# Hybrid decoder, attention stage: two value sums of a head in one PSUM bank, evacuated together

## The chip, the cores and the metric

One core of one Trainium2 chip runs the whole program. The metric is the device time of one execution in microseconds (us). PE is TensorE, DVE is VectorE, ACT is ScalarE, POOL is GpSimd, SP is SyncE, which here issues nearly all transfers.

## What is computed

Two decoder layers on 1024 tokens of width 1024. In each layer one input projection feeds four token mixers of 256 columns; their outputs `y` go through one output projection and a layer norm, then a SwiGLU and a second layer norm. Two of the mixers, a dilated sliding-window attention (c) and a latent attention (b), are computed as masked softmax attention, four heads each:

```
y_a = _gmlp_mixer(z_a, ...)
y_b = _mla_mixer(z_b, positions, ...)
y_c = _dilated_mixer(z_c, positions)
y_d = _mlstm_mixer(z_d, ...)
y = jnp.concatenate([y_a, y_b, y_c, y_d], axis=-1) @ w_out[l]
x = _layer_norm(DEEPNORM_ALPHA * x + y, ln1_g[l], ln1_b[l])
...
s = jnp.where(key_pos[None, :] <= q_pos[:, None], s, -jnp.inf)
p = jax.nn.softmax(s, axis=-1).astype(v.dtype)
return jnp.einsum('bhqk,bkhd->bqhd', p, v)
```

## The kernel before

Float32 products are made from two parts, a rounded high part and the remainder (`PH` and `PL`, `wh` and `wl`): ACT casts the high part, DVE or POOL subtracts it.

`attn` treats four head pairs in turn: `G[0]`, `G[1]` are the heads of mixer c, `G[2]`, `G[3]` those of mixer b. For each head (`hh`) and each block of 128 queries (`i`), `scores` makes score tiles `sc` on PE; DVE adds the mask while it reduces (L824, `P` and `mn`); ACT takes the exponential (L828); POOL scales by the reciprocal of the sum (L831). `turn` transposes `P` on PE (`pt`) and splits it (ACT `PH`, DVE `PL`). `values` makes the value sum `pv` of a block of 256 queries (`jp`, 0 to 3) on PE. The blocks come in the order jp 0, 3, then 1, 2, with jp 0 or 1 first and its partner soon after. The rows 0 to 63 of `pv` come from the high part of V, the rows 64 to 127 from the remainder.

What becomes of `pv` differs by pair:

- `G[0]` to `G[2]`: ACT copies it to `tmp` (L886, 128x256) and SP sends its two halves to `yp` in HBM (L889, 64 KB each).
- `G[3]`: ACT copies the upper half (L883, 64x256) and DVE adds the lower half from PSUM into `Yb` (L884, 64x256).

PSUM has 8 banks of 512 columns: 3 carry the tag `mm`, 2 `s` (scores), 3 `t` (transposes). Tiles of a tag take its banks in turn. Under `mm` stand `pv`, the projections `pkb` and `pqb` that make keys and queries of the next pairs (`kst`, `q`) within the attention, and `po` of the output projection. A tile can be written only when all readers of the bank's last tile are done.

`out_proj` follows. `ysplit` brings the mixers' outputs back: for g = 0 and 3 it loads `yr` from `ys` (L1192), for g = 1 and 2 it loads both parts from `yp` (L1199), and DVE adds them (L1202, `yr<-yr`). ACT and POOL or DVE split each into `yT` (L146, L149). The `yr` tiles, and the raw tiles of `wO` ahead of them, share two buffers (pool `r`), so a load waits until the tile two before it has been split. `proj` then makes `po` in eight tiles of 128 tokens for each half of the columns.

The order on PE within the attention is as the code is written; the order on DVE, ACT, POOL and SP, and everything in `out_proj`, is set by the framework's scheduler from what each step costs and what it hands on, and so can move when an instruction is merged.

Of the kernel before, what the change touches and what calls it, by code (L numbers as in the profile page):

```python
# [11 lines left out]
ALU = mybir.AluOpType  # L12
# [46 lines left out]
class Net:  # L59
# [740 lines left out]
    def attn(self, groups):  # L800

        nc = self.nc

        rows = [(G, jp, hh, 2 * jp + e) for G in groups for two in ((0, 3), (1, 2)) for hh in range(2) for e in range(2) for jp in two]
        P_, PHL, norms = {}, {}, []

        def scores(n):
            G, jp, hh, i = rows[n]
            kst, q1, q2 = G["qk"]
            mask, scale, R, QR, pp = G["mask"], G["scale"], G.get("R"), G.get("QR"), G["pp"]  # L810
            nk = (i + 1) * 128
            qs = slice(i * 128, (i + 1) * 128)
            P = P_[n] = self.u("P", F32, pp[n % len(pp)])
            mn = self.sm("mn", 4)
            nch = (nk + 511) // 512
            for ch in range(nch):
                k0, k1 = ch * 512, min(nk, ch * 512 + 512)
                sp = self.psum("sc", "s")
                pairs = [(q1[hh][:, qs], kst[hh][:, k0:k1]), (q2[hh][:, qs], kst[hh][:, k0:k1])]
                if R is not None:  # L820
                    pairs.append((QR[i // 4][:, hh, (i % 4) * 128:(i % 4) * 128 + 128], R[:, k0:k1]))
                self.mms(sp[:, 0:k1 - k0], pairs)
                m0 = (7 - i) * 128 + k0
                nc.vector.tensor_tensor_reduce(out=P[:, k0:k1], in0=sp[:, 0:k1 - k0], in1=mask[:, m0:m0 + k1 - k0], scale=-scale,  # L824
                                               scalar=mn[:, ch - 1:ch] if ch else 3.0e38, op0=ALU.add, op1=ALU.min, accum_out=mn[:, ch:ch + 1])
            m = mn[:, nch - 1:nch]
            rs = self.sm("rs", 2)
            nc.scalar.activation(P[:, 0:nk], P[:, 0:nk], AF.Exp, scale=-1.0, bias=m, accum_out=rs[:, 0:1])  # L828
            def norm():
                nc.vector.reciprocal(rs[:, 1:2], rs[:, 0:1])  # L830
                nc.gpsimd.tensor_scalar(out=P[:, 0:nk], in0=P[:, 0:nk], scalar1=rs[:, 1:2], scalar2=1.0, op0=ALU.mult, op1=ALU.mult)  # L831
            norms.append(norm)
            while len(norms) > NLAG:
                norms.pop(0)()

        def turn(n):
            G, jp, hh, i = rows[n]
            key = (id(G), jp, hh)
            full = G["full"][jp]
            if i % 2 == 0:  # L840
                ng = (2 * jp + 5) // 4
                PHL[key] = [[self.u(s, F32 if full else F32R, "w").rearrange("p (b n) -> p b n", b=4) for _ in range(ng)] for s in (("PT",) if full else ("PH", "PL"))]
            P = P_.pop(n)
            for b0 in range(0, i + 1, 4):
                k = min(4, i + 1 - b0)
                pt = self.psum("pt", "t")
                for b in range(k):
                    nc.tensor.transpose(pt[:, b * 128:(b + 1) * 128], P[:, (b0 + b) * 128:(b0 + b + 1) * 128], self.ident)  # L848
                c0 = (i % 2) * 128
                src = pt[:, 0:k * 128].rearrange("p (b n) -> p b n", b=k)  # L850
                dst = [Pt[b0 // 4][:, 0:k, c0:c0 + 128] for Pt in PHL[key]]
                if full:
                    G["turns"] = G.get("turns", 0) + 1
                    (nc.scalar.copy if full[G["turns"] % len(full)] == "A" else nc.vector.tensor_copy)(dst[0], src)
                else:
                    self.split(*dst, src)

        def values(n):
            G, jp, hh, i = rows[n]
            V = G["V"]  # L860
            full = G["full"][jp]
            nb = 2 * jp + 2
            pv = self.psum("pv", "mm")
            pairs = PHL.pop((id(G), jp, hh))
            if "heads" in G:
                v = lambda b: V[b // 2][:, b % 2, G["heads"] + hh, :]
            elif full:
                v = lambda b: V[2][:, b, hh * 64:(hh + 1) * 64]
            else:
                v = lambda b: V[hh][:, b, :]  # L870
            m = 64 if full else 128
            for b in range(nb):
                c0 = 128 if b == nb - 1 else 0
                for x, Pt in enumerate(pairs):
                    nc.tensor.matmul(pv[0:m, c0:256], lhsT=v(b), rhs=Pt[b // 4][:, b % 4, c0:256],  # L875
                                     start=b == 0 and x == 0, stop=b == nb - 1 and x == len(pairs) - 1)
            tmp = self.t2("tmp", 256)
            if "Y" in G:
                y = G["Y"][64 * hh:64 * hh + 64, jp * 256:(jp + 1) * 256]
                if full:  # L880
                    nc.scalar.copy(y, pv[0:64, 0:256])
                else:
                    nc.scalar.copy(tmp[0:64, :], pv[0:64, 0:256])  # L883
                    nc.vector.tensor_tensor(out=y, in0=tmp[0:64, :], in1=pv[64:128, 0:256], op=ALU.add)  # L884
                return
            nc.scalar.copy(tmp[0:m, :], pv[0:m, 0:256])  # L886
            for part in range(2):
                dst = G["spill"][part][64 * hh:64 * hh + 64, jp * 256:(jp + 1) * 256]
                nc.sync.dma_start(dst, self.io["c_zero"][:, 0:256] if full and part else tmp[64 * part:64 * part + 64, :])  # L889

        NG = 16
        with self.tc.manual_schedule(engines=MAN):
            s = 0

            def ahead(n):
                nonlocal s
                while s < len(rows) and s <= n + rows[s][0]["ahead"]:
                    if s % NG == 0:
                        self.fill(999)
                        rows[s][0]["start"]()  # L900
                    scores(s)
                    left = sum(r[3] + 1 for r in rows[s:s - s % NG + NG])
                    self.fill(-(-len(self.jobs) * (rows[s][3] + 1) // left))
                    s += 1

            ahead(-1)
            for n in range(len(rows) + VLAG):
                m = n - VLAG
                for x in SEQ:
                    if x == "s":  # L910
                        ahead(n)
                        if s == len(rows):
                            while norms:
                                norms.pop(0)()
                    elif x == "t" and n < len(rows):
                        turn(n)
                    elif x == "v" and m >= 0 and rows[m][3] % 2 == 1:
                        values(m)
# [863 lines left out]
```

## Time and profile before

| what | value |
|---|---|
| time before, median of 3 runs (lowest to highest) | 2399.78 us (2398.84 to 2403.02) |
| the profiled execution, its own time | 2400.5 us |
| its span, mean granted clock of TensorE | 2398.8 us, 0.996 |
| PE busy | 2346.0 us (98%) |
| DVE, POOL, ACT busy | 1612.9 (67%), 1176.9 (49%), 1004.8 (42%) us |
| attention, first layer | 279 to 437 us of the span |
| attention, second layer | 1475 to 1633 us |

The span is the stretch from the first to the last instruction. The shares are means over stages: PE is near its end of what it can do over the whole, but not in the two attention stretches. [...]

### The profile page before, as it was taken

The numbers are of one execution on the slowest core, as the hardware profiler recorded it, in microseconds if no ns is written. First come the engines' busy times: TensorE is split into PE (matmuls) and PEld (weight loads), VectorE is DVE, ScalarE is ACT, GpSimd is POOL, SyncE is SP. The second block draws the span as 40 slices with busy tenths as digits, with TensorE's granted clock in tenths as the row PEclk, the third lists the DMA queues.
The fourth block names the chain that finished last, engine by engine and source line by source line (L and its number), as shares of the span: only waits on it lengthen the run. The fifth ranks groups of instructions, "written<-read, shape, count | busy, mean of one in ns | idle before, by whom it ended". The sixth has DMA issues, their size and how long they took to land.

```text
span 2398.8 us, 33440 instructions
## 1 busy us (share of the span) xinstructions
PE 2346.0 (98%) x11804; PEld 1971.7 (82%) x11804; DVE 1612.9 (67%) x2925; ACT 1004.8 (42%) x2004; POOL 1176.9 (49%) x1097
## 2 busy tenths in 40 slices
PE   9999999999999999999999999999999999999998
PEld 9789878777888888888897898788778888888886
DVE  7743588478765566767957435784787665667689
ACT  6323578334332323544343225783343323235442
POOL 2223525373545455767622244253735455547676
PEclk9999999999999999999999999999999999999999
DMA  4201112522332324653222110135213333345521
GB/s 169 65 29 43 31 37 83 186 110 70 115 114 87 113 99 170 216 189 101 93 66 64 36 37 31 38 87 188 110 62 114 116 102 107 108 164 208 189 97 70
DMA packets 91446, 246.81 MB, mean 103 GB/s; under 512 B 12096, under 2 KB 18560, under 8 KB 91280
## 3 DMA queue, kind: packets, MB, share of 16 engines
q1 hardware_dynamic: 91280, 244.68, 30.1%
q8 instruction: 94, 1.54, 0.3%
q14 instruction: 72, 0.59, 0.1%
HBM read 180.64 MB, written 64.52 MB: 102 GB/s over the span
## 4 chain that ended last, share of the span: by engine, by line
PE 82%; DVE 9%; issue 3%; ACT 3%; POOL 2%; DMA 1%; SPq 0%; POOLq 0%; ACTq 0%; DVEq 0%
PE gu L124 34%; PE dn L124 14%; PE zc L124 6%; PE po L124 5%; PE zvo L572 4%; PE zdq L524 3%; PE za L124 3%; PE zb L124 3%; PE pv L875 2%; PE sc L124 2%; PE dl L124 2%; DVE P L824 1%; PE pt L848 1%; DVE x L1136 1%; DVE PL L149 1%
## 5 line engine op out<-in xcount | busy, mean ns | idle before, releaser
L124 PE MATMUL gu<-T,fc 128*128 128x512 f32 x2640 | 625.9, 395 | 5.1 <-DVE T L1374 5.1
L124 PEld LDWEIGHTS gu<-T,fc 128*128 128x128 f32 x2640 | 496.7, 188 | 123.3 <-DVE T L1374 6.6
L1279 POOL TENSOR_TENSOR fc<-fw,fc 128x512 fp32r<-128x512 f32 x232 | 325.5, 1406 | 348.8 <-ACT fc L1278 341.9
L124 PE MATMUL dn<-dc,dc 128*128 128x512 f32 x1512 | 352.2, 395 | 0.0
L124 PEld LDWEIGHTS dn<-dc,dc 128*128 128x128 f32 x1512 | 283.7, 188 | 68.3 <-DVE dc L1279 1.0
L1278 ACT CAST fc<-fw 128x512 fp32r<-128x512 f32 x232 | 142.8, 620 | 349.5 <-PE gu L124 218.5
L124 PE MATMUL gu<-B,fc 128*128 128x512 f32 x1056 | 260.0, 396 | 0.0
L124 PEld LDWEIGHTS gu<-B,fc 128*128 128x128 f32 x1056 | 197.6, 188 | 46.6
L149 POOL TENSOR_TENSOR dc<-hr,dc 128x512 fp32r<-128x512 f32 x126 | 190.1, 1520 | 79.4 <-ACT dc L146 69.9
L1437 DVE TENSOR_TENSOR Ra<-Ra,gu 128x512 f32<-128x512 f32 x172 | 117.6, 684 | 118.6 <-PE gu L124 101.8
L831 POOL TENSOR_SCALAR P<-P,rs 128x256 f32<-128x256 f32 (+7 forms) x128 | 95.8, 752 | 152.4 <-DVE rs L830 94.9
L124 PE MATMUL po<-wh,yT 128*128 128x512 f32 x512 | 163.2, 397 | 0.6 <-DVE x L1218 0.6
L124 PE MATMUL zc<-wh,xT 128*128 128x384 f32 x512 | 134.1, 339 | 0.0
L1278 ACT CAST dc<-dr 128x512 fp32r<-128x512 f32 x108 | 67.0, 622 | 129.9 <-PE dn L124 75.1
L124 PEld LDWEIGHTS po<-wh,yT 128*128 128x128 f32 x512 | 95.8, 188 | 23.4 <-DVE x L1218 1.5
L124 PE MATMUL sc<-kst,q 128*128 128x512 f32 (+3 forms) x384 | 107.7, 375 | 6.7 <-DVE mn L824 6.6
L828 ACT ACTIVATE P<-P,mn 128x256 f32<-128x256 f32 (+7 forms) x128 | 99.9, 782 | 21.4 <-DVE mn L824 19.8
L1279 DVE TENSOR_TENSOR dc<-dr,dc 128x512 fp32r<-128x512 f32 x72 | 81.1, 1136 | 35.4 <-ACT dc L1278 35.4
L149 DVE TENSOR_TENSOR PL<-pt,PH 128x512 fp32r<-128x512 f32 (+3 forms) x176 | 95.6, 557 | 12.3 <-ACT PH L146 11.8
L140 POOL TENSOR_TENSOR wl<-raw,wh 128x768 fp32r<-128x768 f32 (+2 forms) x32 | 62.6, 1962 | 79.6 <-ACT wh L132 79.1
L124 PE MATMUL po<-wl,yT 128*128 128x512 f32 x256 | 100.7, 395 | 0.0
L848 PE MATMUL pt<-ident,P 128*128 128x128 f32 x576 | 89.2, 281 | 11.4 <-DVE PL L149 5.7
(393 smaller groups left out, 4896.3 us busy)
## 6 DMA issues: line engine op xcount, KB each, us to landing
fw<-in_wGU SPq DMA_DIRECT2D x88, 512.0 KB, 4.6
hr<-hs SPq DMA_DIRECT2D x142, 256.0 KB, 2.8
dr<-in_wD SPq DMA_DIRECT2D x44, 512.0 KB, 5.2
hs<-Ra SPq DMA_DIRECT2D x40, 512.0 KB, 2.9
hs<-Rb SPq DMA_DIRECT2D x22, 512.0 KB, 5.5
raw<-in_wO SPq DMA_DIRECT2D x16, 512.0 KB, 3.6
x<-x SPq DMA_DIRECT2D x16, 512.0 KB, 2.6
raw<-in_wC SPq DMA_DIRECT2D x16, 384.0 KB, 3.0
```

Source lines behind the costliest of these rows:

```text
L124: self.nc.tensor.matmul(out, lhsT=a, rhs=b, start=first and j == 0, stop=last and j == n - 1)
L140: (eng or nc.gpsimd).tensor_sub(lo[:, :n], raw[:, :n], f32(hi[:, :n]))
L149: (lo_eng or nc.vector).tensor_sub(lo, src, f32(hi))
L524: step(lambda: nc.tensor.matmul(pz, lhsT=a, rhs=b_, start=n == 0, stop=n == 23))
L572: nc.tensor.matmul(box["p"], lhsT=a, rhs=b_, start=j == 0, stop=j == 23)
L828: nc.scalar.activation(P[:, 0:nk], P[:, 0:nk], AF.Exp, scale=-1.0, bias=m, accum_out=rs[:, 0:1])
L831: nc.gpsimd.tensor_scalar(out=P[:, 0:nk], in0=P[:, 0:nk], scalar1=rs[:, 1:2], scalar2=1.0, op0=ALU.mult, op1=ALU.mult)
L848: nc.tensor.transpose(pt[:, b * 128:(b + 1) * 128], P[:, (b0 + b) * 128:(b0 + b + 1) * 128], self.ident)
L875: nc.tensor.matmul(pv[0:m, c0:256], lhsT=v(b), rhs=Pt[b // 4][:, b % 4, c0:256], start=b == 0 and x == 0, stop=b == nb - 1 and x == len(pa ...
L1278: nc.scalar.copy(dst[:, 0:512], src)
L1279: lo_eng.tensor_sub(dst[:, 512:1024], src, f32(dst[:, 0:512]))
L1437: tt = lambda o, a, b, op: v.tensor_tensor(out=o, in0=a, in1=b, op=op)
```

## The change

For `G[1]`, `G[2]` and `G[3]` the first block of a head (jp 0 or 1) writes the columns 0 to 255 of a new `pv` tile and returns; its partner (jp 3 or 2) writes the columns 256 to 511 of the same tile and evacuates both: one ACT copy of 512 columns, then two transfers of 64x2x256 (`G[1]`, `G[2]`) or one DVE add of 64x512 (`G[3]`). For one layer these are 12 tiles in place of 24, 12 ACT copies in place of 24, 16 transfers of 128 KB in place of 32 of 64 KB, and 4 DVE adds in place of 8. `G[0]` stays as it is.

```
-            pv = self.psum("pv", "mm")
+
+            both = not any(G["full"])
+            if both:
+                second = jp >= 2
+                if not second:
+                    open_pv[0] = self.psum("pv", "mm")
+                pv = open_pv[0][:, 256 * second:256 * second + 256]
+            else:
+                pv = self.psum("pv", "mm")
...
+            if both:
+                if not second:
+                    return
+                pv, tmp = open_pv[0], self.t2("tmp")
+                blocks = lambda x: x.rearrange("p (j n) -> p j n", n=256)
+                if jp == 3:
+                    at = lambda x: blocks(x)[:, 0:4:3, :]
+                else:
+                    at = lambda x: blocks(x)[:, 1:3, :]
+                if "Y" in G:
+                    nc.scalar.copy(tmp[0:64, :], pv[0:64, :])
+                    nc.vector.tensor_tensor(out=at(G["Y"][64 * hh:64 * hh + 64, :]), in0=blocks(tmp[0:64, :]), in1=blocks(pv[64:128, :]), op=ALU.add)
+                    return
+                nc.scalar.copy(tmp, pv)
+                for part in range(2):
+                    nc.sync.dma_start(at(G["spill"][part][64 * hh:64 * hh + 64, :]), blocks(tmp[64 * part:64 * part + 64, :]))
+                return
             tmp = self.t2("tmp", 256)
-            if "Y" in G:
-                y = G["Y"][64 * hh:64 * hh + 64, jp * 256:(jp + 1) * 256]
-                if full:
-                    nc.scalar.copy(y, pv[0:64, 0:256])
-                else:
-                    nc.scalar.copy(tmp[0:64, :], pv[0:64, 0:256])
-                    nc.vector.tensor_tensor(out=y, in0=tmp[0:64, :], in1=pv[64:128, 0:256], op=ALU.add)
-                return
```

Three places show how it moves instructions. The first is DVE near the end of the first layer's attention, where the first `yr<-yr` add stands (`P`, `mn`: the score reductions; the line L1202 of before is L1219 of after). Of before:

```order
L884 TENSOR_TENSOR Yb_4021<-tmp_4806,pv_4801 64x256
L149 TENSOR_TENSOR PL_4810<-pt_4811,PH_4809 128x128
L824 ISA P_4815,mn_4816<-sc_4817,maskB_4019 128x384
L824 ISA mn_4816 128x1
L1202 TENSOR_TENSOR yr_5203<-yr_5203 128x512
L830 RECIPROCAL rs_4797<-rs_4797 128x1
L830 RECIPROCAL rs_4822<-rs_4822 128x1
L884 TENSOR_TENSOR Yb_4021<-tmp_4843,pv_4826 64x256
L824 ISA P_4863,mn_4864<-sc_4865,maskB_4019 128x512
L824 ISA mn_4864 128x1
```

and of the changed kernel at the same place:

```order
L149 TENSOR_TENSOR PL_4767<-pt_4768,PH_4766 128x128
L1219 TENSOR_TENSOR yr_5147<-yr_5147 128x512
L824 ISA P_4772,mn_4773<-sc_4774,maskB_4005 128x384
L824 ISA mn_4773 128x1
L830 RECIPROCAL rs_4757<-rs_4757 128x1
L896 TENSOR_TENSOR Yb_4007<-tmp_4799,pv_4761 64x2x256
L830 RECIPROCAL rs_4779<-rs_4779 128x1
L824 ISA P_4819,mn_4820<-sc_4821,maskB_4005 128x512
L824 ISA mn_4820 128x1
```

The add of `yr` now stands ahead of the reduction of 384 columns (`P_4815` of before, `P_4772` of after). The second is POOL at the same time, where the scalings of `P` and the remainders of the first two `yT` stand. Of before:

```order
L831 TENSOR_SCALAR P_4760<-P_4760,rs_4767 128x256
L149 TENSOR_TENSOR yT_5197<-yr_5195,yT_5197 128x512
L149 TENSOR_TENSOR yT_5200<-yr_5195,yT_5200 128x512
L831 TENSOR_SCALAR P_4785<-P_4785,rs_4797 128x1024
L831 TENSOR_SCALAR P_4815<-P_4815,rs_4822 128x384
```

and now:

```order
L831 TENSOR_SCALAR P_4720<-P_4720,rs_4727 128x256
L831 TENSOR_SCALAR P_4745<-P_4745,rs_4757 128x1024
L831 TENSOR_SCALAR P_4772<-P_4772,rs_4779 128x384
L149 TENSOR_TENSOR yT_5141<-yr_5139,yT_5141 128x512
L149 TENSOR_TENSOR yT_5144<-yr_5139,yT_5144 128x512
```

Both scalings, of 1024 and of 384 columns, now stand ahead of the two remainders. The next add, of the `yr` that is loaded after those remainders, stands on DVE where it stood, ahead of the reduction of `P_4909` of before, which is `P_4865` of after:

```order
L149 TENSOR_TENSOR PL_4805<-pt_4858,PH_4803 128x4x128
L1219 TENSOR_TENSOR yr_5156<-yr_5156 128x512
L824 ISA P_4865,mn_4866<-sc_4867,maskB_4005 128x512
L824 ISA mn_4866 128x1
L1219 TENSOR_TENSOR yr_5159<-yr_5159 128x512
L824 ISA P_4865,mn_4866<-sc_4872,maskB_4005,mn_4866 128x256
```

In the second layer the same add stands behind both reductions of that `P` (here `P_15859`) and ahead of the next one, of 384 columns:

```order
L824 ISA P_15859,mn_15860<-sc_15866,maskB_14999,mn_15860 128x256
L824 ISA mn_15860 128x1
L1219 TENSOR_TENSOR yr_16150<-yr_16150 128x512
L149 TENSOR_TENSOR PL_15881<-pt_15882,PH_15880 128x3x128
L824 ISA P_15888,mn_15889<-sc_15890,maskB_14999 128x384
L824 ISA mn_15889 128x1
```

The third place is PE at the change from the attention to the output projection, from the end of the last `pv`. Of before:

```order
L875 MATMUL pv_5131<-PL_5088,V_3333 128x256
L875 MATMUL pv_5131<-PH_5086,V_3333 128x128
L875 MATMUL pv_5131<-PL_5088,V_3333 128x128
L124 MATMUL po_5262<-wh_5169,yT_5197 128x512
L124 MATMUL po_5262<-wl_5170,yT_5197 128x512
L124 MATMUL po_5262<-wh_5169,yT_5197 128x512
```

and now:

```order
L883 MATMUL pv_5067<-PL_5036,V_3333 128x256
L883 MATMUL pv_5067<-PH_5034,V_3333 128x128
L883 MATMUL pv_5067<-PL_5036,V_3333 128x128
L124 MATMUL po_5234<-wh_5113,yT_5141 128x512
L124 MATMUL po_5234<-wl_5114,yT_5141 128x512
L124 MATMUL po_5234<-wh_5113,yT_5141 128x512
```

Of before, the tile `po_5262` that follows the last `pv` takes the bank of `pv_5119`, the last but one; the last one's bank is taken by `po_5290`, which begins 26 rows after it. Now `po_5178` and `po_5206` have begun ahead, in the other two banks, and `po_5234`, in the row behind the last `pv`, takes that tile's own bank.

## Rows read from the trace of the kernel before

**Rows 1.** The page, part 1: busy us, share of the span, instructions.

```profile
PE 2346.0 (98%) x11804; PEld 1971.7 (82%) x11804; DVE 1612.9 (67%) x2925; ACT 1004.8 (42%) x2004; POOL 1176.9 (49%) x1097
```

**Rows 2.** Windows: length, busy us (instructions) by engine, granted clock, DMA share, GB/s.

```profile
279.00:437.00 158.00, 142.55 (x962) 122.87 (x960) 132.13 (x399) 126.32 (x298) 70.74 (x89) 0.99 0.19 53
1475.00:1633.00 158.00, 143.75 (x960) 123.91 (x958) 131.27 (x398) 125.90 (x295) 70.22 (x89) 0.98 0.19 53
```

**Rows 3.** Waits of PE, 338 to 463 us: us in total, times, longest.

```profile
PE sc L124 <- DVE mn L824: 3.3, 8, 1.5
PE pt L848 <- DVE PL L149: 2.8, 4, 1.0
PE pv L875 <- DVE q L797: 1.6, 2, 1.2
```

**Rows 4.** The tile pv: its copies and adds, ns min/median/max.

```profile
L886 ACT COPY tmp<-pv x48: 348/370/430, 290.3 to 1604.9; 128x256 f32<-128x256 f32 x40, 64x256 f32<-64x256 f32 x8
L883 ACT COPY tmp<-pv x16: 346/366/369, 413.8 to 1639.0; 64x256 f32<-64x256 f32 x16
L884 DVE TENSOR_TENSOR Yb<-tmp,pv x16: 422/424/425, 415.1 to 1639.4; 64x256 f32<-64x256 f32 x16
```

**Rows 5.** Groups kept apart by shape, 279 to 463 us: busy us, mean ns.

```profile
L787 ACT CAST kst<-pkb 64x512 fp32r<-64x512 f32 x4 | 2.3, 577 | 0.0
L790 DVE TENSOR_TENSOR kst<-pkb,kst 64x512 fp32r<-64x512 f32 x4 | 2.8, 693 | 0.1
```

**Rows 6.** Transfers: count, KB each, median us to landing.

```profile
yp<-tmp SPq DMA_DIRECT2D x88, 64.0 KB, 2.0
yr<-yp SPq DMA_DIRECT2D x5, 512.0 KB, 4.2
```

**Rows 7.** Timeline of PE and of DVE around 359 us: start, us.

```profile
359.34 0.96 PE L124 MATMUL pkb<-kvT,wk 128*128 128x512 f32 x3
...
359.20 0.69 DVE L790 TENSOR_TENSOR kst<-pkb,kst 64x512 fp32r<-64x512 f32 x1
```

**Rows 8.** Timeline of DVE, 415 to 423 us; in brackets idle before, releaser.

```profile
415.81 0.55 DVE L824 CUSTOM_DVE_ANT_0 P<-sc,maskB 128x384 f32<-128x384 f32 x1
...
417.85 0.69 DVE L1202 TENSOR_TENSOR yr<-yr 128x512 f32<-128x512 f32 x1 [1.49 <-POOL yT L149]
...
422.66 0.69 DVE L1202 TENSOR_TENSOR yr<-yr 128x512 f32<-128x512 f32 x1
```

**Rows 9.** Timeline of PE, 419 to 425 us.

```profile
419.92 0.73 PE L124 MATMUL sc<-kst,q 128*128 128x512 f32 x2 [1.46 <-DVE mn L824]
...
421.95 0.63 PE L848 MATMUL pt<-ident,P 128*128 128x128 f32 x4 [0.62 <-DVE PL L149]
...
424.67 0.62 PE L124 MATMUL sc<-kst,q 128*128 128x384 f32 x2 [0.27 <-DVE mn L824]
```

**Rows 10.** Timelines of POOL and of SP's queue, 415 to 420 us.

```profile
415.08 2.57 POOL L149 TENSOR_TENSOR yT<-yr,yT 128x512 fp32r<-128x512 f32 x2
418.79 1.68 POOL L831 TENSOR_SCALAR P<-P,rs 128x1024 f32<-128x1024 f32 x2 [1.15 <-DVE rs L830]
...
417.67 0.37 SPq L1199 DMA_DIRECT2D yr<-yp  x1
```

**Rows 11.** Timelines of PE, ACT and DVE where the output projection begins.

```profile
442.22 0.45 PE L124 MATMUL po<-wh,yT 128*128 128x512 f32 x1
...
442.42 0.37 ACT L883 COPY tmp<-pv 64x256 f32<-64x256 f32 x1 [0.90 <-PE pv L875]
...
442.81 0.42 DVE L884 TENSOR_TENSOR Yb<-tmp,pv 64x256 f32<-64x256 f32 x1 [1.61 <-ACT tmp L883]
```

**Rows 12.** Timeline of PE at the SwiGLU's begin, and the window from there.

```profile
569.35 3.92 PE L124 MATMUL gu<-T,fc 128*128 128x512 f32 x9 [1.94 <-DVE T L1374]
...
569.00:572.00 3.00, 2.65 (x6) 2.15 (x7) 3.00 (x5) 2.80 (x3) 0.00 (x0) 0.56 0.02 5
```

**Rows 13.** Timeline of ACT: the exponential of the 384 columns.

```profile
416.46 0.61 ACT L828 ACTIVATE P<-P,mn 128x384 f32<-128x384 f32 x1
```

More of the change, by code (lines that the diff above doesn't have):

```diff
@@ L804, in attn @@
         rows = [(G, jp, hh, 2 * jp + e) for G in groups for two in ((0, 3), (1, 2)) for hh in range(2) for e in range(2) for jp in two]
-        P_, PHL, norms = {}, {}, []
+        P_, PHL, norms, open_pv = {}, {}, [], [None]
         def scores(n):
```

## Prediction

> **What bounds the kernel now.** I read the page's busy shares first, then the windows of the attention stage, then what PE waits for there, then the timelines of the four engines around those waits. PE is busy for 2346.0 of 2398.8 us [rows 1], so all its idle time is 53 us, and only in the attention is there much of it in one place: 158 us with 142.6 busy in the first layer, 143.8 in the second [rows 2], that is 15.4 and 14.3 us idle. DVE is at 132 and ACT at 126 of those 158 us, so both run close behind PE; POOL, at 71, has room. From 338 us of the first layer on the named waits are for score reductions (3.3 us), for split transposes (2.8) and for the banks that `pqb` held until DVE had read them (1.6) [rows 3]. None of them is for a copy of `pv` or for its transfers. So the engine time that the change saves lies beside PE's work, and the time must come from where a bank comes free and from what stands ahead of what in a queue.
>
> **What is removed.** ACT: a copy takes 0.37 us whether on 128 or on 64 rows [rows 4]; the nearest thing of 512 columns from PSUM is the cast of keys, 0.58 [rows 5]. So 12 pairs save 12 x (2 x 0.37 - 0.58) = 1.9 us of ACT in a layer. DVE: two adds of 0.42 [rows 4] become one, by the subtraction on 64x512 from PSUM 0.69 [rows 5]: 4 x 0.15 = 0.6 us. Since both engines have idle time (26 and 32 us of the 158) and no named wait ends in a `pv` copy, I take nothing for these; if that cover were gone they would be worth at most 2.5 us a layer. The transfers are 16 fewer. One of 64 KB lands 2.0 us after its issue [rows 6], and what it writes is read by loads that wait for a buffer and not for it (one was issued at 417.67, when POOL's work on the buffer's last tile, 2.57 us from 415.08, had just ended [rows 10]). So this too is nothing; if the 2.0 us of each of the 32 transfers stood on the path, 64 us would go, and no named wait is for one [rows 3].
>
> [...]
>
> **What the merged tile does to the banks.** Three banks serve `pv`, `pkb`, `pqb` and `po`. With half the `pv` tiles the turn of the banks changes. By the tiles' order two reuses of before that came close behind a copy fall away in each layer; no named wait of PE ends in such a copy, so I take an estimate of 0.1 us for each, -0.4 in all, the hand-over and little more. The two `q` waits stay, since their tiles keep the predecessor and the distance. One new tight place appears: the first of `pkb` at 359.34 now takes the bank of the `pkb` before it, whose last reader on DVE ran from 359.20 to 359.89 [rows 7]. That is 0.55 and a hand-over less what PE was late anyway: +0.5 a layer, +1.0 in all (bounds 0 and 1.2).
>
> At the output projection the shared tile costs more. Of before, PE goes from the last `pv` to `po` at 442.22 without a wait, since that bank had been read earlier; the last copy ran from 442.42 for 0.37, the add from 442.81 for 0.42 [rows 11], beside PE's work. Now `po_5234`, in the row behind the last `pv`, takes that very bank: it waits for a copy of 0.58 and an add of 0.69 [rows 5] and three hand-overs of some 0.04 (442.42 + 0.37 to 442.81 shows one): 1.4 us, in each layer, +2.8. The other bound is 0, if PE is late there for another reason, by as much.
>
> [...]
>
> **What moves on DVE and POOL.** Before, DVE stood idle 1.49 us until the first `yr` from `yp` had landed, and added it from 417.85; the reduction of 384 columns, 0.55 us, had been done at 415.81 [rows 8]. Now that reduction stands behind the add, and the merged `Yb` add is 0.27 longer than the one there. So the next reduction of 512 columns, for which PE waited until 419.92 [rows 9], is 0.8 late; and with a further reduction now ahead of the second split, the transposes at 421.95 [rows 9] by 1.2.
>
> The larger part comes behind it. The exponential of the 384 columns takes 0.61 [rows 13] and can start only at about 419.1 (417.85 + 0.69 + 0.55), its reciprocal on DVE waits for the `Yb` add, so it is there at about 420.0 and the scaling on POOL ends at 420.7 (1024 and 384 columns took 1.68 together [rows 10], so some 0.6 for this one). Only then come the remainders of the first two `yT`, 2.57 us, which ran from 415.08 before [rows 10]: they end at about 423.4 in place of 417.65. They free the `r` buffer for which the next load waits; SP issued it at 417.67, at once behind them [rows 10], and now issues it at 423.4. It lands 4.2 us later [rows 6], at 427.6 in place of 421.9. Before, its add at 422.66 [rows 8] found it there. Now DVE stands still until 427.6, then adds (0.69) and reduces 512 columns (about 0.7), and PE, which waited for that reduction until 424.67 [rows 9], goes on at about 428.9. That is +4.2 in the first layer, the 1.2 within it. What is queued behind the add on DVE: two reductions, then splits; the exponentials on ACT and all of PE wait for these. The bounds are 0.8, if the load comes in time, and 4.2.
>
> In the second layer the first hold is the same (+1.2), but the late add stands behind both reductions of that block and only ahead of the one of 384 columns, for which PE has two `pv` blocks of other work ahead. I take +1.2, bounds 0 and 4.2.
>
> **What is given back.** After a stall ACT and DVE have caught up, so later waits shorten: the longest for a split, 1.0 us, at the end of the attention [rows 3], once a layer, and part of the 1.94 us before the SwiGLU's first matmul [rows 12], if the layer norm has slack ahead of it. I take -2.5, between 0 and -3.9.
>
> **Sum.** 4.2 + 1.2 + 2.8 + 1.0 - 0.4 - 2.5 = +6.3 us on the profiled 2400.5, so 2406.8; the median shown is 0.7 below that execution, so 2406 us. A measurement of this kernel tells about 0.2%, 4.8 us, from no change: slower is above 2404.6, faster below 2395.0.
>
> **Rivals.**
> No measurable change: the stalls stay but are hidden, since DVE and ACT catch up and the layer norm's slack takes the bank wait. With the first layer at 1.2 and the full -3.9: 1.2 + 1.2 + 2.8 + 1.0 - 0.4 - 3.9 = +1.9, or 2401.7. For it: a single load that is earlier by 3 us decides it, as it has just slack of 0.8 now (landed 421.9, added 422.66). Against it: the order of the rows on POOL and DVE is fixed in the program, whatever the times.
>
> Faster: ACT and DVE are what PE trails in the attention, and what they are spared comes back one for one: 2 x (1.9 + 0.6) = 5.0 and 0.4 of banks, with no new wait: -5.4, or 2394.4. For it: 6.1 of the named waits are for DVE [rows 3]. Against it: those waits end in a reduction or a split that has just been fed, not at the end of a backlog, and the three new waits would all have to fail to come; it decides only if `yr` and the output projection's bank are both hidden. That the transfers themselves were on the path (-64 us, 2336) has a chance under 0.01, since no wait named is for one [rows 3], and is counted here.
>
> Much slower: TensorE's clock. Behind the wait of 1.94 us at 569.35 the granted clock was 0.56 over 3.0 us [rows 12], that is at the lower of its levels for most of it, and 3.0 x 0.44 = 1.3 us were lost; behind the waits of 1.46 and 0.62 at 419.92 and 421.95 [rows 9] PE was not slowed. With some 3 us more of idleness there, and a wait at the output projection, it may be: one or two such stretches, +1.3 to +2.6, and less given back, +8 to +11: 2408 to 2411.
>
> **How the numbers follow.** I give my forecast 0.50, of which 0.10 would be under the 4.8 us; no measurable change 0.28; faster 0.10; much slower 0.12. So faster 0.10, same 0.38, slower 0.52. The range runs from 2397.5, where the bank relief counts and little is lost, to 2411.5; the forecast's own range is 2403 to 2409.
>
> **What would show it.** In the changed profile: PE at about 428.9 behind a wait of some 3 us for `mn` in the first layer, with the load of `yr` issued at about 423.4 and DVE idle until it lands; in the second layer no such wait of over 1.5 us. At the output projection a wait of 1.4 us of `po` for the `Yb` add, in both layers. At 359 us a wait of 0.5 of `pkb` for `kst`. ACT with 24 instructions fewer, and 16 transfers fewer a layer, without PE any shorter in 279 to 404 us. I am wrong if the load of `yr` is issued near 418 again, if PE finds the last bank free, or if PE's idle time before 404 us falls by more than 1 us.

## The result, and the profile after

The changed kernel takes 2419.56 us (median of 4 runs, 2417.62 to 2422.42) against 2401.09 of the kernel before, run beside it: a ratio of 1.0078, 95% interval 1.0061 to 1.0096. It is 18.5 us slower. Forecast were 6 us, with a range that ended at 2411.5.

Both kernels issue the same 11804 matmuls, so a difference in PE's busy time is read here as one of the clock at which they ran (the mean granted clock of the profiled executions was 0.992 for 0.996); the rest of the span is idle time. This row of the page of the changed kernel (span 2420.7 us) answers to [rows 1]:

```profile
PE 2353.7 (97%) x11804; PEld 1977.7 (82%) x11804; DVE 1606.2 (66%) x2917; ACT 1003.8 (41%) x1980; POOL 1182.6 (49%) x1097
```

Idle time (span less PE's busy time) went from 52.8 to 67.0 us, +14.2; busy time rose by 7.7. Together that is 21.9 us between these two executions; the medians are 18.5 apart. The windows of the two attention stages (the second one shifted by the 15 us that the first layer had lost) answer to [rows 2], with the same columns:

```profile
279.00:437.00 158.00, 139.00 (x893) 118.63 (x893) 124.52 (x373) 118.59 (x268) 67.13 (x85) 0.95 0.19 53
1490.00:1648.00 158.00, 140.82 (x926) 120.52 (x924) 127.87 (x382) 120.92 (x275) 67.92 (x86) 0.97 0.19 53
```

The granted clock is lower in both (0.95 and 0.97 for 0.99 and 0.98), and DVE and ACT did less work in the same length. What PE waited for from 338 to 474 us shows three new names, `x`, `Yb` and `pkb`, beside those of [rows 3] (us in total, times, longest):

```profile
PE pt L848 <- DVE PL L149: 5.9, 5, 2.4
PE sc L124 <- DVE mn L824: 4.9, 8, 1.3
PE po L124 <- DVE x L1235: 3.4, 1, 3.4
PE po L124 <- DVE Yb L896: 1.4, 1, 1.4
PE pkb L124 <- DVE kst L790: 0.6, 1, 0.6
```

Two of the three places that the prediction priced are there to 0.1 us: 0.57 for `pkb`, 1.39 for the bank behind the last `pv`. The timeline of PE has each with its releaser in brackets (compare [rows 7, 9, 11]):

```profile
361.75 1.62 PE L124 MATMUL pkb<-kvT,wk 128*128 128x512 f32 x3 [0.57 <-DVE kst L790]
...
425.12 0.73 PE L124 MATMUL sc<-kst,q 128*128 128x512 f32 x2 [0.94 <-DVE mn L824]
...
428.91 0.63 PE L848 MATMUL pt<-ident,P 128*128 128x128 f32 x4 [2.38 <-DVE PL L149]
...
433.78 1.01 PE L124 MATMUL sc<-kst,q 128*128 128x384 f32 x2 [1.35 <-DVE mn L824]
...
456.96 0.50 PE L124 MATMUL po<-wh,yT 128*128 128x512 f32 x1 [1.39 <-DVE Yb L896]
...
473.33 0.51 PE L124 MATMUL po<-wh,yT 128*128 128x512 f32 x1 [3.40 <-DVE x L1235]
```

**At the end of the attention** the timelines of DVE and POOL answer to [rows 8, 10]:

```profile
422.17 0.69 DVE L1219 TENSOR_TENSOR yr<-yr 128x512 f32<-128x512 f32 x1 [2.02 <-issue]
422.78 0.55 DVE L824 CUSTOM_DVE_ANT_0 P<-sc,maskB 128x384 f32<-128x384 f32 x1
...
426.13 0.69 DVE L824 CUSTOM_DVE_ANT_0 P<-sc,maskB 128x512 f32<-128x512 f32 x1 [0.19 <-PE sc L124]
...
426.75 1.55 DVE L149 TENSOR_TENSOR yT<-yr,yT 128x512 fp32r<-128x512 f32 x1
428.22 0.88 DVE L149 TENSOR_TENSOR PL<-pt,PH 128x384 fp32r<-128x384 f32 x2
...
432.43 0.69 DVE L1219 TENSOR_TENSOR yr<-yr 128x512 f32<-128x512 f32 x1 [1.54 <-DMA yr<-yp]
...
423.58 1.68 POOL L831 TENSOR_SCALAR P<-P,rs 128x1024 f32<-128x1024 f32 x2 [4.38 <-DVE rs L830]
425.23 2.52 POOL L149 TENSOR_TENSOR yT<-yr,yT 128x512 fp32r<-128x512 f32 x2
```

The order is as foretold: the add of `yr`, then the reduction of 384 columns, POOL's scalings, and then its two remainders, to 427.75; the next load was issued at 428.32 (4 to 5 us of the shift are from ahead of this place), and DVE stood idle 1.54 us for it at 432.43. What was not foreseen is the row at 426.75: a remainder of `yT` on DVE took 1.55 us in place of 0.68, to 428.30, and the splits behind it are what PE waited 2.38 us for. It also held the load. From 405 to 440 us SP's queue had these two waits before a load of `yr` from `yp` (us in total, times, longest), the first in the kernel before, the second in the changed one:

```profile
SPq L1199 <- POOL yT L149: 3.6, 1, 3.6
...
SPq L1216 <- DVE yT L149: 6.2, 1, 6.2
```

So the load that goes first waited for DVE's remainder now, in the second layer too (issued at 1635.87), and not for POOL's two.

**At the output projection** these are the rows of ACT, DVE and SP's queue:

```profile
455.61 0.58 ACT L895 COPY tmp<-pv 64x512 f32<-64x512 f32 x1 [5.94 <-PE pv L883]
456.94 0.62 ACT L146 CAST yT<-Yb 128x512 fp32r<-128x512 f32 x1 [0.76 <-DVE Yb L896]
457.47 1.14 ACT L146 CAST yT<-yr 128x512 fp32r<-128x512 f32 x2
...
456.22 0.69 DVE L896 TENSOR_TENSOR Yb<-tmp,pv 64x512 f32<-64x512 f32 x1 [5.77 <-ACT tmp L895]
...
471.87 0.69 DVE L1219 TENSOR_TENSOR yr<-yr 128x512 f32<-128x512 f32 x1 [13.58 <-DMA yr<-yp]
472.59 1.88 DVE L1235 SCALAR_TENSOR_TENSOR x<-x,po 128x512 f32<-128x512 f32 x3
...
459.50 0.33 SPq L1209 DMA_DIRECT2D yr<-ys  x1
...
468.07 7.99 SPq L1216 DMA_DIRECT2D yr<-yp  x3
```

The add for `Yb` starts at 456.22, behind the copy of the last tile; the cast of `Yb` behind it at 456.94; only then the casts of two `yr`, whose buffers the next loads need. These are issued at 459.50 and, for `yp`, at 468.07; their add on DVE at 471.87 comes after 13.58 us of idle time, and behind it stand the three `x<-x,po` that free the banks for PE: 3.40 us of waiting. In the kernel before, block 1 and block 2 were evacuated apart, so the first half of `Yb` was ready with block 1, before the last `pv` had ended. In the second layer PE waits 0.31 us there: the scheduler has put the three `x<-x,po` ahead of the add, in the first layer behind it. DVE in the second layer, to be compared with 471.87 and 472.59 above:

```profile
1675.02 1.88 DVE L1235 SCALAR_TENSOR_TENSOR x<-x,po 128x512 f32<-128x512 f32 x3 [11.23 <-PE po L124]
1677.86 0.69 DVE L1219 TENSOR_TENSOR yr<-yr 128x512 f32<-128x512 f32 x1 [0.96 <-issue]
```

**The clock.** Three windows of the changed kernel (length, busy us by engine, granted clock, DMA share, GB/s) show a granted clock of 0.50 to 0.66 after waits. In slices of 0.5 us the traces of both kernels read 1.00 or 0.50, and a value between only in the first and last slice of a slow stretch; where a lower level of the clock is spoken of, it is this 0.50:

```profile
322.00:327.00 5.00, 5.00 (x14) 3.03 (x14) 0.50 (x3) 1.54 (x5) 0.99 (x1) 0.50 0.00 0
429.00:437.00 8.00, 6.65 (x31) 6.06 (x32) 5.18 (x16) 2.71 (x6) 2.09 (x3) 0.57 0.38 131
473.00:477.00 4.00, 3.67 (x11) 2.86 (x12) 3.87 (x7) 0.83 (x3) 0.00 (x0) 0.66 0.32 97
```

The first of them lies behind waits of 1.33, 0.68 and 0.48 us that the change did not make: the kernel before has 1.33, 0.68 and 0.61 at the same place, and a granted clock of 1.00 from 322 to 327 us. So not all of the lost clock can be put down to the added waits.

### The profile page after: what moved, and what is told of

It is laid out like the page before. It is cut to its first block, busy times and chain, and to the rows that moved or that the text cites. A ratio compares the mean times of both kernels' runs of the same rounds, so it can differ in the third digit from the quotient of the medians.

```text
span 2420.7 us, 33339 instructions
## 1 busy us (share of the span) xinstructions
PE 2353.7 (97%) x11804; PEld 1977.7 (82%) x11804; DVE 1606.2 (66%) x2917; ACT 1003.8 (41%) x1980; POOL 1182.6 (49%) x1097
## 3 DMA queue, kind: packets, MB, share of 16 engines
q8 instruction: 94, 1.54, 0.3%
```

## The experiments

Fifteen runs, timed beside the kernel before in the same batch unless marked as a single run. "Idle" is the span less PE's busy time, in the profiled execution; before has 2398.8, 2346.0 and 52.8.

| kernel | median us (before beside it) | ratio, 95% interval | span, PE busy, idle |
|---|---|---|---|
| the change | 2419.56 (2401.09) | 1.0078 [1.0061, 1.0096] | 2420.7, 2353.7, 67.0 |
| e1, all but the last pair | 2408.30 (2400.35) | 1.0032 [1.0022, 1.0043] | 2407.4, 2349.9, 57.5 |
| e2, the last pair only | 2414.71 (2400.35) | 1.0061 [1.0048, 1.0073] | 2415.0, 2350.3, 64.7 |
| e3, bank shared, evacuated apart | 2412.31 (2400.35) | 1.0049 [1.0037, 1.0062] | 2408.8, 2348.6, 60.2 |
| e4, own banks, merged transfers | 2399.97 (2400.35) | 1.0000 [0.9991, 1.0009] | 2398.2, 2345.4, 52.8 |
| e5, the change, loads in order 0, 2, 3, 1 | 2416.76 (2400.83) | 1.0068 [1.0056, 1.0081] | 2414.9, 2350.7, 64.2 |
| e6, before, loads in order 0, 2, 3, 1 | 2398.37 (2400.83) | 0.9990 [0.9981, 0.9998] | 2396.7, 2343.6, 53.1 |
| e7, the change, last tile apart | 2411.48 (2400.83) | 1.0049 [1.0035, 1.0063] | 2409.6, 2349.1, 60.5 |
| e8, the second pair only | 2401.28 (2400.83) | 1.0010 [1.0001, 1.0019] | 2397.0, 2343.0, 54.0 |
| e9, the change, two loads in pool B | 2413.61 (2400.64) | 1.0049 [1.0036, 1.0061] | 2412.7, 2350.9, 61.8 |
| e10, before, two loads in pool B | 2400.09 (2400.64) | 0.9997 [0.9988, 1.0006] | 2399.6, 2345.6, 54.0 |
| e11, the change again (single run) | 2418.75 | | 2417.0, 2350.1, 66.9 |
| e12, before again (single run) | 2399.10 | | 2397.4, 2345.7, 51.7 |
| e13, the change, remainder on POOL | 2424.55 (2400.16) | 1.0097 [1.0084, 1.0110] | 2422.7, 2353.6, 69.1 |
| e14, e7 with the remainder on POOL | 2412.87 (2400.16) | 1.0048 [1.0035, 1.0060] | 2405.6, 2347.3, 58.3 |
| e15, e8 in the order 0, 2, 3, 1 | 2403.39 (2400.16) | 1.0006 [0.9997, 1.0015] | 2402.4, 2347.0, 55.4 |

**Which pairs, and which part of the edit (e1 to e4).** e1 leaves the last pair as before, e2 changes it alone:

```
-            both = not any(G["full"])
+            both = not any(G["full"]) and "Y" not in G        # e1
+            both = "Y" in G                                   # e2
```

> Value sums share a bank in the second and third head pair only; the last pair, whose sums go to Yb, is as before. Theory A (the loss comes from the last pair: its sums of blocks 1 and 2 arrive together, so Yb is ready later at the output projection, the last bank is held, and the loads of yr behind it are late): PE's wait of 1.39 us for the Yb add and that of 3.40 for x are gone, the remainders of yT on POOL stand ahead of the scalings as before, and the waits for split transposes near 429 and 1636 us shrink from 2.38 to under 1; what stays is 0.5 us a layer for pkb and 1 us for the add of yr ahead of a reduction, and clock stretches: 2402 to 2406 us. Theory B (shared banks in the attention themselves cost, by holding a bank for two blocks): 8 of 12 pairs still share, so two thirds of the 18.5 us stay: 2411 to 2415 us.

> Value sums share a bank in the last head pair only. Theory A: the wait of about 1.4 us for the Yb add is there in both layers, and the late loads of yr with some 3 us for x in the first; no wait for pkb at 361 us: 2411 to 2417 us. Theory B: 4 of 12 pairs, a third of the loss: 2406 to 2408 us.

e1 came out at +8.0 us, above theory A's 2402 to 2406 and under theory B's range; e2, with a third of the tiles, at +14.4, as theory A had it and twice what theory B gave. So the last pair costs most; the two parts do not add up to the whole (8.0 + 14.4 for 18.5). Its two waits are there, 1.39 and 3.53 us in the first layer; in the second they are 1.39 and 3.42, where the change has 0.31.

e3 keeps the shared bank, and copies, adds and sends the halves apart once both are done; e4 keeps the banks apart and merges the transfers of the second and third pair alone:

```
+                for c, j in ((0, 3 - jp), (1, jp)):           # e3, per half
+                    nc.scalar.copy(tmp, pv)
...
+                nc.scalar.copy(tmp[:, 256 * second:256 * second + 256], pv[:, 0:256])    # e4
+                if second:
...
+                        nc.sync.dma_start(at(G["spill"][part][64 * hh:64 * hh + 64, :]), blocks(tmp[64 * part:64 * part + 64, :]))
```

> All three pairs share the bank as in the change, but after the second block each half is copied, added and sent apart, as before (24 copies, 32 transfers of 64 KB, 8 adds a layer). If the loss comes from the shared bank and from both blocks being ready together (theory A or B), it stays: 2414 to 2421 us, and the last bank is held about 0.3 us longer than 1.39, for two copies and two adds. If it comes from the longer single instructions and merged transfers (theory C), it goes: 2399 to 2404 us.

> Each block has its own bank and its own copy, as before; in the second and third pair the two copies go to halves of one tile, which is sent with 2 transfers of 128 KB in place of 4 of 64 KB. It tells what the transfers alone are worth. Theories A and B: nothing waits for them, 2399 to 2403 us, the same as before. Theory C: part of the loss, over 2405 us.

e3 stays at +12.0, a little under the range for A or B and far above theory C's: some two thirds of the loss come with the shared bank alone. Its wait for the `Yb` add is 1.86 us (for 1.39), as two copies and two adds stand in a row. The rest does not stay: idle time is 60.2 for 67.0, and the wait of 3.40 for `x` is 0.32 in both layers, since in e3 the three `x<-x,po` stand ahead of the add of `yr` on DVE. e4 is the same as before, with the same idle time of 52.8: 16 transfers fewer a layer are worth nothing, nor do they cost anything. Theory C is out as the whole cause, but some 6 us go with the merged instructions and the order that the scheduler gives them; no run parts these two.

**The last tile (e7).** Of the 12 tiles of a layer only the last is taken back:

```
-            both = not any(G["full"])
+            both = not any(G["full"]) and not ("Y" in G and hh == 1 and jp in (1, 2))
```

> The change, but in the last pair the second head's blocks 1 and 2, the last tile of the attention, are kept in banks of their own and evacuated apart: 11 of 12 tiles a layer are shared. Theory A (at the output projection the loss comes from this one tile: it holds the last bank, and makes the first half of Yb wait for block 2, behind which the casts of yr, their buffers and the next loads stand): the waits of 1.39 us for the Yb add and of 3.40 for x in the first layer are gone, with the clock stretch behind the latter: 6 to 8 us less than the change, 2411 to 2414. What stays is in the attention (order of DVE and POOL, pkb, clock). Theory B (the shared banks in general): 11 of 12 of the loss, 2417 to 2419.

It measured 2411.5, within theory A's range: this one tile is 8 of the 18.5 us. Its timeline of PE has the 2.38 near the end of the attention still, and at the output projection only the 0.32 that the kernel before had at 479.70:

```profile
426.13 0.63 PE L848 MATMUL pt<-ident,P 128*128 128x128 f32 x4 [2.38 <-DVE PL L149]
...
487.98 0.50 PE L124 MATMUL po<-wh,yT 128*128 128x512 f32 x1 [0.32 <-DVE x L1240]
```

**The second pair alone (e8).**

```
+            both = not any(G["full"]) and "heads" not in G
```

> Value sums share a bank in the second head pair only (mixer c's heads 3 and 4): 4 tiles a layer, 8 transfers fewer, 4 copies fewer. No pkb tile for a next pair takes a bank of a late reader, and the order at the end of the attention is that of before. Theory A: no loss, 2397 to 2402 us, since a shared bank as such costs nothing. Theory B: a third of e1 and e2 together, 2406 to 2408.

Within the range: +0.4 us by the medians, and a ratio of 1.0010 (2.4 us) whose interval just leaves out no change. But the expectation was wrong on one point: the wait for `pkb` is there, so it comes from the second pair's tiles, which shift the turn of the banks, and not from the third's:

```profile
358.47 0.95 PE L124 MATMUL pkb<-kvT,wk 128*128 128x512 f32 x3 [0.56 <-DVE kst L790]
```

So a shared bank as such, with its wait of 0.56 us a layer, costs some 1 us of idle time (54.0 for 52.8). The third pair's part, by e1 less e8, is 7 us, of which the profiled executions show 3.5 as idle time (57.5 for 54.0) and the rest as clock: e1's end of attention has DVE's add of `yr` ahead of the reduction of 384 columns, as the change has it, and e8 has it as before.

**What holds the output projection (e5, e6).** For the first half of the tokens the loads come in another order, with `Yb` last:

```
-            for g in range(4):
+            for g in ((0, 2, 3, 1) if h == 0 else range(4)):
```

> The change, but the first half of the tokens loads its mixers' outputs in the order 0, 2, 3, 1, so that Yb's part comes last and no load of yr stands behind it. PE still waits for the last bank (1.4 us a layer). Theory A: the wait of 3.40 us for x in the first layer is gone, and so is the hold of POOL's two remainders on the second load ahead of a reduction in part, as that load now feeds nothing that is due at once: 2411 to 2416 us. If the loads of yr are not what held x, the 3.4 us stay: 2418 to 2421.

> The kernel before with that same order of the loads, 0, 2, 3, 1: a control for e5. Nothing stood behind Yb for long there, so I expect 2397 to 2403 us, no measurable difference; if the order of the loads is worth something by itself, e5 must be compared with this and not with before.

The wait of 3.40 for `x` is gone in e5, and the 2.38 is 0.92, as the long remainder on DVE has moved; but the time, 2416.8, is only 2.8 lower and just above the range: a split at 433.18 now waits 2.55 us, in the second layer two wait 2.38 and 2.76. The wait for the last bank, foretold as 1.4 in each layer, was 0.41 in the first and 1.39 in the second. e6 shows that the order is harmless to the kernel before, 2.5 us to the good. That is the fastest kernel of the study, with an interval that just leaves out no change, but within the 0.2% that a measurement tells; e15, which adds the second pair's shared tiles to it, did not keep it.

> The best two edits together: bank shared in the second head pair only (e8), and the order 0, 2, 3, 1 of the loads (e6). The shared tiles there are worth nothing, so as e6: 2396 to 2401 us.

Measured 2403.4, above its range, 1.0006 with an interval that holds no change: nothing here beats the kernel before by more than can be told.

**What makes the waits at the end of the attention (e9, e10, e13, e14).** e9 gives the two loads behind the remainders buffers of their own, e10 does so in the kernel before:

```
-                        raw = self.uw("yr", F32, "r")
+                        raw = self.u("yr", F32, "B") if g == 2 and h == 0 else self.uw("yr", F32, "r")
```

> The change, with the two loads of yr of the first token half that feed the third mixer part (g = 2) in two tiles of pool B, which has room there, so that they wait for no remainder on POOL; the scheduler then sets their adds behind the last Yb add on DVE, out of the attention. If the hold on DVE by that late load is what costs at the end of the attention, the waits of 2.38 and 1.35 us near 429 and 434, and 2.38 near 1636, fall to under 1 each and those behind them shrink: some 4 us less in the first layer and 2.5 in the second; the loads behind it come earlier too, so that the wait of 3.40 for x goes. PE's wait for the last bank (1.39 a layer) stays: 2406 to 2412 us. If the waits come from the added reductions and splits themselves, 2415 to 2420.

> The kernel before with the same two loads in pool B: the control for e9. There the second load was in time for its add, so only the three adds move away from the reductions: 2395 to 2401 us.

e9 came to 2413.6, above its range but below the other. The waits of 1.35 and of 3.40 are gone, so loads that wait for a buffer made these; the 2.38 stayed at 2.37, against what was expected. e10 is the same as before, as expected, so the larger pool by itself does nothing. The rows of e9, between which PE has no wait where the change has its 1.35:

```profile
428.48 0.63 PE L848 MATMUL pt<-ident,P 128*128 128x128 f32 x4 [2.37 <-DVE PL L149]
...
437.55 0.73 PE L124 MATMUL sc<-kst,q 128*128 128x512 f32 x2 [0.71 <-DVE mn L824]
```

e13 moves the remainder that took 1.55 us, and that of the first half of `Yb`, from DVE to POOL, e14 does that in e7:

```
-                    self.split(t[:, 0, :], t[:, 1, :], y[f], lo_eng=nc.vector if g == 1 else nc.gpsimd)
+                    self.split(t[:, 0, :], t[:, 1, :], y[f], lo_eng=nc.vector if g == 1 and h == 1 else nc.gpsimd)
```

> The change, with the remainders of yT of the first token half that DVE subtracts (g = 1, 128x512, both operands from SBUF) given to POOL, where those of g = 0, 2 and 3 are. In the change this DVE instruction took 1.55 us in place of 0.68 while POOL's two remainders ran, ahead of the split that PE waited 2.38 us for. If that instruction, lengthened by POOL, is what makes the wait, it falls to under 1.2 us in both layers and the whole by 2 to 4 us: 2415 to 2418 us. If the reductions ahead of the split are, it stays above 2 and the time at 2418 to 2421.

> The same edit on e7 (the last tile apart): both of the main causes taken away, 11 of 12 tiles a layer still shared. If they are the causes, some 2 to 4 us less than e7's 2411.5: 2407 to 2410 us; the rest above before is the add of yr ahead of a reduction, the waits behind pkb, and clock stretches. If it falls to 2403 or below, little else is lost; if it stays at 2411, the wait behind DVE's remainder was hidden anyway.

In both the wait is 0.92 in place of 2.38, in both layers: DVE's remainder made it. But e13 as a whole is slower than the change, 2424.6, against both ranges: POOL now has three remainders in a row, the loads of the output projection come later still, and PE waits elsewhere:

```profile
426.48 0.63 PE L848 MATMUL pt<-ident,P 128*128 128x128 f32 x4 [0.92 <-DVE PL L149]
...
435.30 0.73 PE L124 MATMUL sc<-kst,q 128*128 128x512 f32 x2 [1.96 <-DVE mn L824]
...
463.01 0.50 PE L124 MATMUL po<-wh,yT 128*128 128x512 f32 x1 [1.21 <-ACT yT L146]
...
472.40 0.80 PE L124 MATMUL po<-wh,yT 128*128 128x512 f32 x1 [4.92 <-DVE x L1235]
```

e14 has 2.2 us less idle time than e7, and the same time within its runs (2407.3 to 2415.5); its range was missed by 3 us.

**The clock (e11, e12).** Second traces of both kernels:

> The change once more, for a second trace. PE's idle time is set by the program and should be the same 67 us within 1 us, with the same named waits; the stretches at the lower clock level may lie elsewhere and be fewer or more than nine, and the span should move with PE's busy time (2353.7 us in the first trace).

> The kernel before once more, for a second trace: idle time 53 us within 1 us, and two to five stretches at the lower clock level, not all where the first trace had its four.

Idle time came again to 66.9 and 51.7 us, the latter 0.3 outside what was expected. Of the change's named waits the 1.35 was 0.41, the others shown above were the same within 0.2 us. Busy time was 2350.1 (for 2353.7) and 2345.7 (for 2346.0). From 270 to 670 and from 1470 to 1870 us the kernel before has its slow stretches in both traces at the same four places, near 286, 569, 1481 and 1519 us (0.51, 0.57, 0.55 and 0.57 over 3.5 to 4 us of the first trace), where some elsewhere was expected. Those of the change lay partly elsewhere, and partly not: the second trace has none behind the wait for `x`, but one behind the wait for `pkb` of the second layer, at 1568 us (0.50 to 1570); behind the 2.38 of the second layer the first trace has one from 1634 us on (0.57 to 1642), the second has a granted clock of 1.00 from 1630 to 1640. It has again a slow part behind the waits near 425:

```profile
421.00:432.00 11.00, 7.50 (x30) 6.42 (x31) 8.86 (x22) 5.95 (x14) 4.82 (x6) 0.64 0.29 95
```

So the profiled executions are 20 to 22 us apart, some 14 to 15 of it idle time, which came again within 1.1 us for either kernel, and 4 to 8 of clock, which vary from one execution of the change to the next.

## Why the prediction was wrong

The direction, and the places, were right; the size was not, and two mechanisms were wrong or missing. The profiled execution grew by 21.9 us for the 6.3 of the sum: idle time by 14.2, the clock, which the sum put at nothing, took 7.7. Point by point, in idle time of PE, from the timelines of both kernels:

| term | foretold | measured |
|---|---|---|
| end of the attention, first layer | +4.2 | 7.3 for 3.5: +3.7 |
| end of the attention, second layer | +1.2 | 4.8 for 3.2: +1.7 |
| the last bank, both layers | +2.8 | 2 x 1.39: +2.8 |
| `pkb`, both layers | +1.0 | 0.57 + 0.56: +1.1 |
| two tight reuses gone | -0.4 | the waits from 379 to 416 us and their like: +1.9 |
| the loads of `yr` behind `Yb` | not priced | 3.40 for 0.32: +3.1 |
| given back later | -2.5 | 0.0 |
| sum | +6.3 | +14.2 |

**What is removed.** Right: the copies took 3.8 us less of ACT and the adds 1.3 less of DVE in all, as foretold, transfers were fewer, and no gain is seen on PE. e4 shows it for the transfers; for ACT and DVE it is argued from the waits, as no run spares them alone.

**The banks.** Right for the last bank, where the cause is shown by e7. (The row that was to show a hand-over of 0.04 shows 0.02; in the change they measure 0.03 to 0.05.) For `pkb` the price was right; the reduction of 256 columns that follows it is late as well (0.72 for 0.15 in the first layer, and again in the second), also in e8. And a split of the third pair waits 1.06 us for 0.38, in e1 and e7 too and not in e2 and e8. The two take back more than the reuses gave: a term of -0.4 that measured +1.9.

**DVE and POOL.** The order acted as foretold, the hold on the load did not: it waited for DVE's remainder, not for POOL's two. Less the 4.9 us by which PE ran behind ahead of this place it was issued at 423.4, just as foretold; that is luck. The price of the late load was too high (1.35 us in one trace, 0.41 in the other, for some 3), and beside it stood one that I had not seen: DVE's remainder, 1.55 us beside POOL's two where it took 0.68 with POOL idle, and with it a wait of 2.38 us in both layers, 1.8 over that of before, where 1.2 was foretold. That the sum of the term came near in the first layer is luck as well, two errors that cancel.

**The step that failed first** is "what is given back": -2.5 us foretold, 0.0 measured. No slack behind the attention took a stall up: the wait at its end grew from 1.00 to 1.35, and those before the SwiGLU and in the layer norm only changed places (1.94 became 0.44 + 1.41).

**The second** is a term that is missing. Under "what the merged tile does to the banks" I counted only the bank that the last tile holds. The same tile also joins block 1, of the first token half, with block 2, of the second, so that half of `Yb` waits for the other; and behind its cast on ACT stand casts whose buffers the next loads need. The trace of before shows the cast of `Yb` ahead of the last `pv`'s end (it began at 439.86, the last `pv` matmul at 442.10), and DVE's order in the changed kernel has the add of `yr` ahead of the three `x<-x,po` in the first layer; I did not follow them. It takes both: in e3, and in the second layer of the change, the tile is shared but the three stand ahead of the add, and the wait is 0.3 us; in e2, with the add ahead in both layers, it is 3.53 and 3.42.

**The third**, and the largest in the first trace, is the clock, at nothing in the sum. It was the rival "much slower", at 0.12 and with 1.3 to 2.6 us, and it came, at 4.4 to 7.7 us. From [rows 9, 12] I read, by a slow stretch at 569 us and none behind the waits at 420, that longer waits at the end of the attention would mostly be spared, too; in the first layer they were not in either trace of the change, in the second layer in one of two.

The rivals "no measurable change" and "faster" both rested on stalls being hidden, and fall with the first point. Why e14 has 2 us less idle time than e7 and no less time, and e15 is 5 us above e6, stays open; their runs spread over 6 to 8 us, the slower ones at a lower mean granted clock (0.993 to 0.995 for 0.996 to 0.997).

## What to carry to other kernels

Before merging the evacuation of two results, ask who needs the first of them alone: an instruction saved on engines that have room was worth nothing here, and the first result is late by the whole second one, with everything that stands behind its reader in that reader's queue. A tile of the last round is the one to leave apart: taking back one of twelve gave 8 of 18.5 us. Where a scheduler sets the order, read in its output not only what moved ahead of what PE waits for, but also what stands behind each instruction that waits for a load, and do not count on later slack unless a wait there ends on the same engine.

## What the runs showed of the hardware

A subtraction on DVE of 128x512 with both operands in SBUF took 0.68 us while POOL was between instructions (at 474.99 of the changed kernel), and 1.55 us when it began at 426.75, while the second of POOL's two remainders ran from about 426.5 to 427.75; it ended 0.55 us after POOL's. The second layer has the same: 1.55 us from 1634.29, with POOL's remainder done at 1635.29. That it made next to no way until POOL had ended is an estimate from these times. A split of the same size that reads PSUM kept its 0.69 beside POOL's work: at 405.19, while POOL subtracted from 403.89 to 408.99. It goes the other way as well: a remainder on POOL that began at 1681.98, while one on DVE ran from 1681.77 to 1682.45, took 1.63 us, where the one at 1687.16 took 1.29. No run changed POOL's work alone.

PE's time is not a sum of waits: 14 to 15 us more of idle time, spread over waits of 0.5 to 3.4 us, came with 4 to 8 us more of busy time for the same matmuls, by stretches at a granted clock of 0.50 that lie behind such waits, but not behind the same ones in each execution. The execution with the fewest such stretches (e8, two from 270 to 670 and from 1470 to 1870 us, at about 568 and 1763, where before has four; busy 2343.0) was 1.8 us shorter than the profiled one of before, though its idle time was longer by 1.2.
